# Seven of sixteen v units of attention by seven block products, with v ahead of q in two head groups

## The chip, the cores and the metric

One core of a Trainium2 chip runs the whole kernel. The metric is the device time of one execution in microseconds (us), taken as the median of several runs.

## What is computed

A two-layer decoder trunk on 256 tokens of width 2048 in float32: a pooling mixer and a gated feed-forward layer, then attention and a second feed-forward layer, each followed by a layer norm. The change lies in attention. Cut to that:

```python
def dilated_attention(h, k, v, w_q, w_o):
    q = (h @ w_q).reshape(B_, S, N_HEADS, HEAD_DIM)        # 16 heads of 128
    for window, dil in DILATED_BRANCHES:                   # (128, 1), (512, 4), (2048, 16)
        o, lse = _dilated_branch(q, k, v, window, dil)     # softmax over allowed distances
        ...
    wts = jax.nn.softmax(jnp.stack(lses, axis=0), axis=0)
    o = jnp.sum(wts[..., None] * jnp.stack(outs, axis=0), axis=0)
    return o.reshape(B_, S, D_MODEL).astype(h.dtype) @ w_o

# in reference():
k_shared = (h @ shared_w_k).reshape(B_, S, N_HEADS, HEAD_DIM)
v_shared = (h @ shared_w_v).reshape(B_, S, N_HEADS, HEAD_DIM)
```

The kernel merges the three branches into one softmax whose weights count in how many branches a distance is allowed (`cnt`).

## The kernel before

**Units.** All large products are cut into units, kept in the list `units` and numbered by their place in it. A unit is one weight block of 512 x 512 with its matmuls, and perhaps a `post` that takes the finished sums out of PSUM. Every number is split into a high part of the type float32r and a low part, so a block costs three products (high-high, high-low, low-high). The tiles `raw`, `wh` and `wl` of a unit (number behind the name) are the loaded block, its high part, cast by ScalarE (L82), and its low part, subtracted on VectorE (L83).

**What sets the order.** The engines' programs are written out in the order in which `run_units` emits them; nothing is rescheduled. For each unit i it first issues the loads up to unit i + 5 on SP (three `raw` buffers) and the splits up to unit i + 3 (four `wh` and `wl` buffers), then the unit's matmuls, then what was put off with `later(n, ...)` until n units on, then the unit's `post`. Each engine's queue is in order, SP's too: a load or a move that waits holds up what stands behind it.

**Seven products.** In the feed-forward layers many down-projection blocks are done by seven products of half-blocks in place of eight (`mk_seven`, `split_sums`). Such a block is two entries in `units`: half "a" with three products and half "b" with four. It has one load but two splits, the first of which (L103 to L109) also forms sums of the weights in `raw`, the second (L96, L97) splits these. On the left side it needs four sums of blocks of the activations, made by `left_sums`. Its results lie in four PSUM banks, two of which (`s2`, `s3`) are added into the others' output by `early`.

**Attention.** There are four head groups hq of four heads. Before, each takes four units of k, four of q and four of v. `group` makes k and q units, with features on the partitions, `group_tm` makes v units, with tokens on the partitions. `scores` does two heads at a time: q times k on TensorE, then the softmax on VectorE and ScalarE, which gives the probabilities `p`. These have to be turned before they can multiply v. `blocks` does that for a pair of heads: VectorE turns 32 x 32 blocks into `pb` (one buffer), then SP issues sixteen DMAs, eight after each of the next two units, that move the blocks to their places in `pTs`. `outputs` then multiplies `pTs` with `vt`, the finished v, in two PSUM banks, and ScalarE and VectorE take these out to `o`. Head group 3 is turned on TensorE instead (`transposes`). PSUM has eight banks, given out by `bank`.

Of the kernel before, what the change touches and what calls it, by code (L numbers as in the profile page):

```python
# [9 lines left out]
F32 = mybir.dt.float32  # L10
F32R = mybir.dt.float32r
# [6 lines left out]
T = 256  # L18
P = 128
# [13 lines left out]
def trunk(ctx: ExitStack, tc: tile.TileContext, x, pool_w_in, pool_w_grp, pool_scale, pool_w_out,  # L33
# [86 lines left out]
    def later(n, fn):  # L120
        if n == 0:
            fn()
        else:
            pending.append([n, fn])
# [818 lines left out]
    scale = 1.0 / math.sqrt(P)  # L943
    qk, pr, oq, pT, vts = {}, {}, {}, {}, {}

    def v_post(c):
        def post(t, ps):
            if t == 0:
                vts[c] = pools["attn"].tile([P, 2, 512], F32, name="vt", tag="vt")
                A.copy(vts[c][:, 0, :], ps)  # L950
            else:
                V.tensor_copy(vts[c][:, 1, :], ps)
                if c == 3:
                    later(1, lambda: transposes(c, (0, 1)))
                    later(2, lambda: transposes(c, (2, 3)))
                later(2 if c == 3 else 4, lambda: outputs(c, (0, 1)))
                later(3 if c == 3 else 7, lambda: outputs(c, (2, 3)))
        return post

    def qk_post(nm, hq):  # L960
        def post(ps):
            later(2 if hq == 0 and nm == "k" else 0, lambda: evac(ps))

        def evac(ps):
            ap = pools["attn"]
            o = ap.tile([P, 4, T], F32, name=nm, tag=nm)
            qk[nm] = o

            if hq == 0 and nm == "k":
                norm_evac(ps, 4, lambda m: o[:, m, :])  # L970
            else:
                for m in range(4):
                    A.copy(o[:, m, :], ps[m][:, T:])
                    V.tensor_tensor(o[:, m, :], o[:, m, :], ps[m][:, :T], OP.add)
            if nm == "q":
                later(2, lambda: scores(hq, range(0, 2)))
                later(3, lambda: scores(hq, range(2, 4)))
                if hq < 3:
                    later(4, lambda: blocks(hq, (0, 1)))
                    later(7, lambda: blocks(hq, (2, 3)))  # L980
        return post

    def scores(hq, ms):
        ap = pools["attn"]
        for m in ms:
            ps = bank("s")
            q, k = qk["q"][:, m, :], qk["k"][:, m, :]
            PE.matmul(ps[:, 0:P], q[:, :P], k[:, :P], start=True, stop=True)
            PE.matmul(ps[:, P:3 * P], q[:, P:], k, start=True, stop=True)  # L989
# [4 lines left out]
            V.scalar_tensor_tensor(sf, ps[:, :3 * P], scale, nf, op0=OP.mult, op1=OP.add)  # L994
# [25 lines left out]
    def transposes(hq, ms):  # L1020
        t = turned(hq, ms)
        for m in ms:
            ps = bank("pT")
            s = pr.pop((hq, m))[0]
            for i in range(3):
                PE.transpose(ps[:, i * P:(i + 1) * P], s[:, i, :], ident)
            A.copy(t[:, m % 2], ps[:, :3 * P])


    def blocks(hq, ms):  # L1030
        two = pr.pop((hq, ms[0]))[2]
        pr.pop((hq, ms[1]))
        b = hp.tile([P, 6 * P], F32, name="pb", tag="h")
        V.transpose(b, two.rearrange("p h s k -> p (h s k)"))

        t = turned(hq, ms)
        to = t.rearrange("p h s -> p (h s)").rearrange("p (k a j) -> p a k j", k=6, a=4)
        fr = b.rearrange("p (k b j) -> p b k j", k=6, b=4)

        def move(rows):  # L1040
            for i in rows:
                for j in range(4):
                    nc.sync.dma_start(to[32 * j:32 * j + 32, i], fr[32 * i:32 * i + 32, j])

        later(1, lambda: move((0, 1)))
        later(2, lambda: move((2, 3)))

    def outputs(hq, ms):
        if ms[0] == 0:
            oq[hq] = quad_tile("o")  # L1050
        vt = vts[hq]
        for m in ms:
            hd = slice(m * P, (m + 1) * P)
            ps = bank("o")
            t = pT.pop((hq, m))
            PE.matmul(ps[:, :T], vt[:, 0, hd], t[:, :T], start=True, stop=False)  # L1056
            PE.matmul(ps[:, P:T], vt[:, 1, hd], t[:, T:], start=False, stop=True)
            A.copy(oq[hq][:, m, 0, :T], ps[:, :T])
            V.tensor_tensor(oq[hq][:, m, 1, :T], ps[:, :T], oq[hq][:, m, 0, :T].bitcast(F32), OP.subtract)  # L1059
# [150 lines left out]
```

## Time and profile before

| what | value |
|---|---|
| median of 3 runs | 2030.75 us (2029.47 to 2030.89) |
| the profiled execution's own time | 2030.49 us |
| its span, first to last instruction | 2028.6 us |
| TensorE matmul, busy | 2021.7 us, 100% |
| VectorE, busy | 1674.5 us, 83% |
| ScalarE, busy | 1257.2 us, 62% |
| granted TensorE clock, mean | 0.999 |

In the profile PE is TensorE, PEld its weight loads, DVE VectorE, ACT ScalarE, SP the engine that issues most DMAs (SPq its queue). A row of a timeline is: start in us from the span's start, duration in us, engine, line of the source, operation, written tile <- read tiles, shapes, and in brackets the idle time ahead with what ended it. A matmul's duration contains the pipeline, so consecutive matmuls overlap; the distance of their starts is what one costs. A row of groups ends with the count, the total in us and the mean in ns, then idle time ahead. DMA rows give the time from issue to landing.

### The profile page before, as it was taken

The page shows a single profiled execution, that of the slowest core. Times are in us where ns is not written, and L with a number is a line of the kernel's source. Part 1 is how long each engine was busy: PE and PEld are TensorE (multiplying, and loading weights), DVE is VectorE, ACT ScalarE, POOL GpSimd, SP SyncE. Part 2 cuts the span into 40 slices and gives each one's busy share as a digit, 9 for nine tenths or more (in the row PEclk, how much of TensorE's full clock was granted, in tenths as well). Part 3 has the DMA queues.
Part 4 walks back from the last instruction along what each step waited for, and adds up shares of the span by engine and source line. Part 5 has one row for each costly group of instructions (what it writes and reads, how often), then busy time and mean ns, then how long its engine had stood idle before and what let it go on. Part 6 is the DMA issues. An engine that isn't in the chain of part 4 may idle for free.

```text
span 2028.6 us, 31127 instructions
## 1 busy us (share of the span) xinstructions
PE 2021.7 (100%) x12496; PEld 1809.4 (89%) x12496; DVE 1674.5 (83%) x1998; ACT 1257.2 (62%) x1685; POOL 75.0 (4%) x111
## 2 busy tenths in 40 slices
PE   9999999999999999999999999999999999999999
PEld 8898988899889988889888888998899989989987
DVE  6859887899789999879756657787889888989898
ACT  5544686667766676657533444577667676667672
POOL 2000000000000001100000000000000000100100
PEclk9999999999999999999999999999999999999999
DMA  8565467666655757864566554557666756666665
GB/s 257 201 206 188 165 209 210 190 192 225 210 191 187 234 188 219 232 226 165 191 197 195 169 185 168 187 178 216 187 198 197 228 187 213 198 213 196 209 214 180
DMA packets 278305, 405.92 MB, mean 200 GB/s; under 512 B 80414, under 2 KB 95668, under 8 KB 277904
## 3 DMA queue, kind: packets, MB, share of 16 engines
q1 hardware_dynamic: 266144, 389.72, 57.9%
q0 software_dynamic: 11584, 13.55, 4.4%
q8 instruction: 98, 1.61, 0.3%
q10 hardware_dynamic: 432, 0.66, 0.1%
q14 instruction: 47, 0.39, 0.1%
HBM read 380.01 MB, written 2.10 MB: 188 GB/s over the span
## 4 chain that ended last, share of the span: by engine, by line
PE 99%; DMA 0%; SPq 0%; DVE 0%; ACT 0%; issue 0%; DVEq 0%
PE acc L165 43%; PE acc L166 22%; PE t L238 3%; PE t L239 3%; PE t L240 3%; PE acc L169 3%; PE acc L170 3%; PE acc L168 3%; PE s L228 3%; PE s L229 3%; PE s L227 3%; PE t L228 2%; PE t L227 2%; PE t L229 2%; PE s L989 0%; PE o L1056 0%
## 5 line engine op out<-in xcount | busy, mean ns | idle before, releaser
L165 PE MATMUL acc<-xc,wh 128*128 128x512 f32 x3264 | 1151.9, 396 | 0.0
L166 PE MATMUL acc<-xc,wl 128*128 128x256 f32 x3264 | 916.3, 281 | 0.0
L83 DVE TENSOR_TENSOR wl<-raw,wh 128x2048 fp32r<-128x2048 f32 (+2 forms) x320 | 692.4, 2168 | 248.4 <-ACT wh L82 243.9
L165 PEld LDWEIGHTS acc<-xc,wh 128*128 128x128 f32 x3264 | 616.0, 189 | 143.7 <-DVE o L1059 0.6
L82 ACT CAST wh<-raw 128x2048 fp32r<-128x2048 f32 (+2 forms) x320 | 578.1, 1812 | 225.7 <-PE acc L165 118.3
L166 PEld LDWEIGHTS acc<-xc,wl 128*128 128x128 f32 x3264 | 615.5, 189 | 0.5
L96 ACT CAST wh<-raw 128x1024 fp32r<-128x1024 f32 x112 | 117.4, 1053 | 150.2 <-DVE raw L107 134.1
L97 DVE TENSOR_TENSOR wl<-raw,wh 128x1024 fp32r<-128x1024 f32 x112 | 133.8, 1221 | 0.5 <-ACT wh L96 0.5
L103 ACT CAST wh<-raw 128x1024 fp32r<-128x1024 f32 x112 | 87.7, 832 | 41.2 <-PE acc L165 24.7
L106 DVE TENSOR_TENSOR wl<-raw,wh 128x1024 fp32r<-128x1024 f32 x112 | 101.9, 951 | 1.3 <-ACT wh L103 0.9
L586 ACT ACTIVATE c<-u,cv 128x256 f32<-128x256 f32 x172 | 89.5, 593 | 19.4 <-DVE f L649 8.2
L228 PE MATMUL t<-wl,g 128*128 128x256 f32 x328 | 92.2, 281 | 0.0
L227 PE MATMUL t<-wh,g 128*128 128x256 f32 x328 | 92.1, 281 | 0.0
L229 PE MATMUL t<-wh,g 128*128 128x256 f32 x328 | 91.9, 280 | 0.0
L271 POOL DMA_DIRECT2D ht<-w x24 | 20.3, 847 | 1808.1 <-ACT wh L103 1060.1
L577 ACT COPY u<-acc 128x256 f32<-128x256 f32 x164 | 54.0, 372 | 46.9 <-PE acc L166 46.8
L229 PE MATMUL s<-wh,xs 128*128 128x256 f32 x296 | 82.6, 279 | 0.0
L228 PE MATMUL s<-wl,xs 128*128 128x256 f32 x296 | 82.6, 279 | 0.0
L227 PE MATMUL s<-wh,xs 128*128 128x256 f32 x296 | 82.5, 279 | 0.0
L591 ACT ACTIVATE a<-u,cv 128x256 f32<-128x256 f32 x172 | 73.6, 500 | 12.3 <-DVE g L659 6.5
L591 ACT ACTIVATE u<-u,cv 128x256 f32<-128x256 f32 x172 | 73.5, 500 | 0.0
L109 DVE TENSOR_TENSOR raw<-raw 128x1024 f32<-128x1024 f32 x56 | 68.6, 1225 | 1.9
(279 smaller groups left out, 3444.8 us busy)
## 6 DMA issues: line engine op xcount, KB each, us to landing
raw<-in_ffn_w_up_dram SPq DMA_DIRECT2D x160, 1024.0 KB, 4.9
raw<-in_ffn_w_down_dram SPq DMA_DIRECT2D x80, 1024.0 KB, 5.1
raw<-in_pool_w_out_dram SPq DMA_DIRECT2D x16, 1024.0 KB, 5.0
raw<-in_shared_w_k_dram SPq DMA_DIRECT2D x16, 1024.0 KB, 5.1
raw<-in_attn_w_q_dram SPq DMA_DIRECT2D x16, 1024.0 KB, 5.3
raw<-in_shared_w_v_dram SPq DMA_DIRECT2D x16, 1024.0 KB, 5.9
raw<-in_attn_w_o_dram SPq DMA_DIRECT2D x16, 1024.0 KB, 5.0
raw<-in_pool_w_in_dram SPq DMA_DIRECT2D x12, 1024.0 KB, 5.6
```

What stands on the lines that cost most here:

```text
L82: A.copy(wh[i][:, s], r[:, s])
L83: V.tensor_tensor(wl[i][:, s], r[:, s], wh[i][:, s].bitcast(F32), OP.subtract)
L96: A.copy(h[:, :, n], r[:, :, n])
L97: V.tensor_tensor(l[:, :, n], r[:, :, n], h[:, :, n].bitcast(F32), OP.subtract)
L106: V.tensor_tensor(l[:, k, n], r[:, k, n], h[:, k, n].bitcast(F32), OP.subtract)
L165: PE.matmul(ps[m], h[:, k, c], q[:, k, :, :T], start=st, stop=False)
L166: PE.matmul(ps[m][:, :T], l[:, k, c], q[:, k, 0, :T], start=False, stop=sp and not shifted)
L227: PE.matmul(to, xh, h[:, k, n], start=opens and kk == 0, stop=False)
L228: PE.matmul(to, xh, l[:, k, n], start=False, stop=False)
L229: PE.matmul(to, xl, h[:, k, n], start=False, stop=ends and kk == 1)
L586: A.activation(c[:, m, :], u[:, m, 2:], AF.Identity, scale=cv[:, 2, j:j + 1], bias=cv[:, 3, j:j + 1])
L591: A.activation(to[:, m, :], u[:, m, i:i + T], AF.Copy, scale=cv[:, i, j:j + 1])
```

## The change

Seven of the sixteen v blocks (three each in head groups 1 and 2, one in group 3) become seven-product blocks. `v_sums` forms the left sums from the normalised stream H for blocks 1, 2 and 3, once, while head group 1's k runs; the float32 sums lie in the buffer of k, the split ones in two tiles of the pool of activations (`xsum`) and in small tiles. `v_early` puts what lies in the two additional banks into `vt` first, and `v_post` adds the other two. In head groups 1 and 2 the order of the units is k, v, q. The calls of `outputs` move from v's `post` to q's. For head group 1 `blocks` comes 3 and 6 units after q (before: 4 and 7) and `outputs` 10 and 11 units after it (for groups 0 and 2: 8 and 11).

```diff
     def v_post(c):
         def post(t, ps):
-            if t == 0:
-                vts[c] = pools["attn"].tile([P, 2, 512], F32, name="vt", tag="vt")
-                A.copy(vts[c][:, 0, :], ps)
+            v = v_tile(c)[t]
+            if c > 0:
+                V.tensor_tensor(v, v, ps, OP.add)
+            elif t == 0:
+                A.copy(v, ps)
             else:
-                V.tensor_copy(vts[c][:, 1, :], ps)
-                if c == 3:
-                    later(1, lambda: transposes(c, (0, 1)))
-                    later(2, lambda: transposes(c, (2, 3)))
-                later(2 if c == 3 else 4, lambda: outputs(c, (0, 1)))
-                later(3 if c == 3 else 7, lambda: outputs(c, (2, 3)))
+                V.tensor_copy(v, ps)
+            if t == 1 and c == 3:
...
+    def v_early(c):
+        def early(p16, p75):
+            v0, v1 = v_tile(c)
+            left, right = v0[:, :256], v0[:, 256:]
+            A.copy(left, p16[:, :256])
+            V.tensor_tensor(right, left, p16[:, 256:], OP.add)
+            V.tensor_tensor(v1[:, :256], right, p75[:, :256], OP.add)
+            V.tensor_tensor(right, right, p75[:, 256:], OP.add)
+            V.tensor_tensor(v1[:, 256:], v1[:, :256], p75[:, 256:], OP.add)
+        return early
+    def v_sums(q, then):
...
+        f = ap.tile([P, 4, T], F32, name="f", tag="k")
+        d = [f[:, i].rearrange("p (k t) -> p k t", k=2) for i in range(4)]
+        V.tensor_tensor(d[0], a21, a22, OP.add)
+        V.tensor_tensor(d[1], d[0], a11, OP.subtract)
+        V.tensor_tensor(d[2], a21, a11, OP.subtract)
+        V.tensor_tensor(d[3], a12, d[1], OP.subtract)
+        def rest():
+            if q < 3:
+                t = quad_tile("xsum")
+                vsums[q] = [[t[:, i, hl, :T].rearrange("p (k t) -> p k t", k=2) for hl in range(2)] for i in range(4)]
+                split_act(t, f)
+                then()
+                return
...
+        later(1, rest)
...
             if nm == "q":
                 later(2, lambda: scores(hq, range(0, 2)))
+                if hq < 3:
+                    later(4 - (hq == 1), lambda: blocks(hq, (0, 1)))
+                    later(7 - (hq == 1), lambda: blocks(hq, (2, 3)))
+                    later(10 if hq == 1 else 8, lambda: outputs(hq, (0, 1)))
+                    later(11, lambda: outputs(hq, (2, 3)))
                 later(3, lambda: scores(hq, range(2, 4)))
-                if hq < 3:
-                    later(4, lambda: blocks(hq, (0, 1)))
-                    later(7, lambda: blocks(hq, (2, 3)))
+                if hq == 0:
+                    later(4, lambda: v_sums(3, lambda: v_sums(1, lambda: v_sums(2, lambda: None))))
...
+    def v_group(hq):
+        js = (0, 1, 2, 3)
+        seven = {0: (), 1: (1, 2, 3), 2: (1, 2, 3), 3: (3,)}[hq]
+        group_tm(shared_w_v, rows4, 512 * hq, 512, xsrcs, v_post(hq),
+                 seven={j: (lambda j=j: vsums[j]) for j in js if j in seven}, early=v_early(hq))
+
     for hq in range(4):
         x0 = hq == 0
         group(shared_w_k, rows4, 512 * hq, 512, psrcs if x0 else xsrcs, qk_post("k", hq), mode="x" if x0 else "ab")
+        if hq in (1, 2):
+            v_group(hq)
         group(attn_w_q[0], rows4, 512 * hq, 512, xsrcs, qk_post("q", hq))
-        group_tm(shared_w_v, rows4, 512 * hq, 512, xsrcs, v_post(hq))
+        if hq in (0, 3):
+            v_group(hq)
```

Before, head group 1 is the units 206 to 209 (k), 210 to 213 (q) and 214 to 217 (v). Now it is 206 to 209 (k), 210 to 216 (v: 210 plain, then three pairs "a", "b") and 217 to 220 (q); head group 2 is 221 to 224 (k), 225 to 231 (v: 225 plain, then the pairs 226/227, 228/229, 230/231) and 232 to 235 (q).

**VectorE, head group 1's turnings.** `pb` is the turned pair, and `wl` with its number shows where in the units this stands. Before, from the last split ahead of the first turning to the second turning:

```order
L83 TENSOR_TENSOR wl220_10305<-raw220_10180,wh220_10304 128x2048
L1034 STREAM_TRANSPOSE pb_10332<-p_10213 128x768
L952 COPY vt_10335<-t1_10155 128x512
L83 TENSOR_TENSOR wl221_10341<-raw221_10241,wh221_10340 128x2048
L83 TENSOR_TENSOR wl222_10391<-raw222_10302,wh222_10390 128x2048
L83 TENSOR_TENSOR wl223_10437<-raw223_10338,wh223_10436 128x2048
L1034 STREAM_TRANSPOSE pb_10472<-p_10274 128x768
```

Now, the last rows ahead of the second turning (the first stands ahead of the second pair's scores and of the split of 227):

```order
L104 TENSOR_TENSOR raw228_10511<-raw228_10511 128x2x256
L106 TENSOR_TENSOR wl228_10646<-raw228_10511,wh228_10645 128x4x256
L106 TENSOR_TENSOR wl228_10646<-raw228_10511,wh228_10645 128x2x256
L107 TENSOR_TENSOR raw228_10511<-raw228_10511 128x2x256
L109 TENSOR_TENSOR raw228_10511<-raw228_10511 128x4x256
L97 TENSOR_TENSOR wl229_10691<-raw228_10511,wh229_10690 128x4x256 x2
L1090 STREAM_TRANSPOSE pb_10714<-p_10560 128x768
```

Before, the second turning stood behind three plain splits after the first; now it stands behind the two halves of block 228/229, with the score chain of the second pair, the second half of 226/227 and the copies of k ahead of them.

**SP, head group 1's moves and the loads among them** (`pTs` are the moves of one pair, eight in a row; `raw` with its number is a unit's load). Before:

```order
L1043 DMA pTs_10334<-pb_10332 32x6x32 x8
L72 DMA raw224_10388<-in_attn_w_q_dram 128x4x512
L1043 DMA pTs_10334<-pb_10332 32x6x32 x8
L72 DMA raw225_10434<-in_attn_w_q_dram 128x4x512
L72 DMA raw226_10475<-in_shared_w_v_dram 128x4x512
L1043 DMA pTs_10474<-pb_10472 32x6x32 x8
L72 DMA raw227_10541<-in_shared_w_v_dram 128x4x512
L1043 DMA pTs_10474<-pb_10472 32x6x32 x8
```

Now:

```order
L1099 DMA pTs_10556<-pb_10554 32x6x32 x8
L72 DMA raw230_10643<-in_shared_w_v_dram 128x4x512
L1099 DMA pTs_10556<-pb_10554 32x6x32 x8
L72 DMA raw232_10717<-in_attn_w_q_dram 128x4x512
L1099 DMA pTs_10716<-pb_10714 32x6x32 x8
L72 DMA raw233_10760<-in_attn_w_q_dram 128x4x512
L1099 DMA pTs_10716<-pb_10714 32x6x32 x8
L72 DMA raw234_10794<-in_attn_w_q_dram 128x4x512
```

The loads between the moves were those of units 224 to 227; now they are those of v's last pair (230) and of the q units 232 and 233, and load 234 stands behind all moves.

**VectorE, head group 1's outputs taken out of PSUM** (`o` on the right is the PSUM bank; `vt` is v). Before:

```order
L83 TENSOR_TENSOR wl225_10544<-raw225_10434,wh225_10543 128x2048
L83 TENSOR_TENSOR wl226_10594<-raw226_10475,wh226_10593 128x2048
L83 TENSOR_TENSOR wl227_10632<-raw227_10541,wh227_10631 128x2048
L1059 TENSOR_TENSOR o_10513<-o_10667,o_10513 128x256
L1059 TENSOR_TENSOR o_10513<-o_10672,o_10513 128x256
L83 TENSOR_TENSOR wl228_10680<-raw228_10591,wh228_10679 128x2048
```

Now:

```order
L83 TENSOR_TENSOR wl232_10797<-raw232_10717,wh232_10796 128x2048
L83 TENSOR_TENSOR wl233_10827<-raw233_10760,wh233_10826 128x2048
L1115 TENSOR_TENSOR o_10848<-o_10849,o_10848 128x256
L1115 TENSOR_TENSOR o_10848<-o_10854,o_10848 128x256
L83 TENSOR_TENSOR wl234_10862<-raw234_10794,wh234_10861 128x2048
L1115 TENSOR_TENSOR o_10848<-o_10889,o_10848 128x256
L1115 TENSOR_TENSOR o_10848<-o_10894,o_10848 128x256
L972 TENSOR_TENSOR vt_10899<-vt_10899,s2_10656 128x256
```

Before, the second pair's outputs stood three units behind the first pair's, after unit 224 and behind the split of 227. Now the two pairs stand one split apart, after units 230 and 231, the second behind the split of 234, and the additions of v behind both.

More of the change, by code (lines that the diff above doesn't have):

```diff
@@ L958, in v_post @@
-        return post
+            v = v_tile(c)[t]
[3 more added lines that the diff above has]
+                A.copy(v, ps)
+            else:
+                V.tensor_copy(v, ps)
+            if t == 1 and c == 3:
+                later(1, lambda: transposes(c, (0, 1)))
+                later(2, lambda: transposes(c, (2, 3)))
+                later(2, lambda: outputs(c, (0, 1)))
+                later(3, lambda: outputs(c, (2, 3)))
+        return post
@@ new lines, in v_early @@
+    def v_early(c):
[8 more added lines that the diff above has]
+        return early
+    vsums = {}
+    def v_sums(q, then):
+        ap = pools["attn"]
+        x = H[q]
+        a11, a12, a21, a22 = (x[:, k:k + 2, t * P:t * P + P] for k, t in ((0, 0), (2, 0), (0, 1), (2, 1)))
+        f = ap.tile([P, 4, T], F32, name="f", tag="k")
[11 more added lines that the diff above has]
+                return
+            w = lnp.tile([P, 2, T], F32R, name="vs0", tag="fold2")
+            z = ap.tile([P, 2, T], F32R, name="vs3", tag="vs3")
+            vs = [[w[:, 0], w[:, 1]], [z[:, 0], z[:, 1]]]
+            for pair in (("S", "Q"), ("cs", "f1")):
+                vs.append([lnp.tile([P, T], F32R, name=f"vs{nm}", tag=nm) for nm in pair])
+            for i, v in enumerate(vs):
+                A.copy(v[0], f[:, i])
+            for i, v in enumerate(vs):
+                V.tensor_tensor(v[1], f[:, i], v[0].bitcast(F32), OP.subtract)
+            vsums[q] = [[u.rearrange("p (k t) -> p k t", k=2) for u in v] for v in vs]
+            then()
+        later(1, rest)
```

4 lines of the change are left out of this document (added).

## The prediction

> **What bounds the kernel now.** I read the page's busy times and its chain first.
>
> ```profile
> PE 2021.7 (100%) x12496; PEld 1809.4 (89%) x12496; DVE 1674.5 (83%) x1998; ACT 1257.2 (62%) x1685; POOL 75.0 (4%) x111
> PE 99%; DMA 0%; SPq 0%; DVE 0%; ACT 0%; issue 0%; DVEq 0%
> ```
>
> TensorE is never idle and the chain is TensorE alone. So a matmul taken away is worth the distance to the next one's start, and a wait put in front of TensorE costs its full length. The timeline of PE gives these distances: a seven-product unit of the feed-forward layer, a v unit (second and last matmul), a k unit (first matmul, and first of the next), an output block and a score block.
>
> ```profile
> 695.20 0.28 PE L227 MATMUL s<-wh,g 128*128 128x256 f32 x1
> 700.15 0.39 PE L165 MATMUL acc<-xc,wh 128*128 128x512 f32 x1
> ...
> 994.67 0.40 PE L239 MATMUL t<-wl,xc 128*128 128x512 f32 x1
> 999.79 0.39 PE L240 MATMUL t<-wh,xc 128*128 128x512 f32 x1
> 1000.01 0.39 PE L165 MATMUL acc<-xc,wh 128*128 128x512 f32 x1
> 1005.63 0.39 PE L165 MATMUL acc<-xc,wh 128*128 128x512 f32 x1
> 1022.53 0.59 PE L1056 MATMUL o<-pTs,vt 128*128 128x256 f32 x2
> 1024.08 0.28 PE L166 MATMUL acc<-xc,wl 128*128 128x256 f32 x1
> 1059.01 0.38 PE L988 MATMUL s<-k,q 128*128 128x128 f32 x2
> 1060.56 0.39 PE L239 MATMUL t<-wl,xc 128*128 128x512 f32 x1
> ```
>
> Seven products take 42 matmuls in 700.15 - 695.20 = 4.95 us, 0.118 each: 2.12 for the 18 of half "a", 2.83 for the 24 of half "b". A plain v unit takes 22 distances in 999.79 - 994.67 = 5.12, so 24 take 5.59. A k or q unit takes 1005.63 - 1000.01 = 5.62. An output block and a score block take 1.3 each (1.55 less the 0.23 of the matmul inside the bracket).
>
> **What goes.** Seven units at 5.59 - 4.95 = 0.64 us: **4.4 us less** on TensorE. This term is sure, since the same code runs in the feed-forward layer at this rate.
>
> **What comes on VectorE.** A plain unit costs it one subtraction, a seven-product unit eight operations.
>
> ```profile
> L83 DVE TENSOR_TENSOR wl<-raw,wh 128x2048 fp32r<-128x2048 f32 x280 | 640.4, 2289 | 234.5 <-ACT wh L82 230.3 <-DMA pTs<-pb 2.0 <-ACT wgb L444 1.7
> L97 DVE TENSOR_TENSOR wl<-raw,wh 128x1024 fp32r<-128x1024 f32 x112 | 133.8, 1221 | 0.5 <-ACT wh L96 0.5
> L109 DVE TENSOR_TENSOR raw<-raw 128x1024 f32<-128x1024 f32 x56 | 68.6, 1225 | 1.9
> L106 DVE TENSOR_TENSOR wl<-raw,wh 128x1024 fp32r<-128x1024 f32 x56 | 68.2, 1218 | 1.3 <-ACT wh L103 0.9
> L107 DVE TENSOR_TENSOR raw<-raw 128x512 f32<-128x512 f32 x56 | 38.8, 692 | 1.9
> L106 DVE TENSOR_TENSOR wl<-raw,wh 128x512 fp32r<-128x512 f32 x56 | 38.2, 683 | 0.0
> L104 DVE TENSOR_TENSOR raw<-raw 128x512 f32<-128x512 f32 x56 | 38.2, 682 | 0.0
> L286 DVE TENSOR_TENSOR xc<-h,xc 128x1024 fp32r<-128x1024 f32 x12 | 14.6, 1219 | 0.0
> L645 DVE TENSOR_TENSOR f<-c 128x256 f32<-128x256 f32 x17 | 7.1, 418 | 0.0
> L1059 DVE TENSOR_TENSOR o<-o 128x256 fp32r<-128x256 f32 x16 | 6.8, 425 | 22.2 <-ACT o L1058 22.2
> L974 DVE TENSOR_TENSOR k<-k,acc 128x256 f32<-128x256 f32 x12 | 4.2, 412 | 0.0
> L1034 DVE STREAM_TRANSPOSE pb<-p 128x768 f32<-128x768 f32 x6 | 5.8, 975 | 4.4 <-DMA pTs<-pb 4.4
> L82 ACT CAST wh<-raw 128x2048 fp32r<-128x2048 f32 x280 | 533.8, 1908 | 213.6 <-PE acc L165 114.6 <-issue 28.6 <-DMA raw<-in_ffn_w_down_dram 19.7
> ```
>
> Half "a" is 0.68 + 1.22 + 0.68 + 0.69 + 1.23 = 4.50, half "b" 2 x 1.22 = 2.44: 6.94 against 2.29, and more than the 4.95 that TensorE takes for the unit. Three in a row lose 6 us against TensorE; the lead of three units in the queue can hold that by itself. What can't be held is what stands behind it in program order: the turning of the probabilities, and the moves on SP.
>
> **Where TensorE comes to wait.** I set t = 0 at head group 1's first score block, after unit 222 (1059.01 in the trace of before). TensorE then has: score block to 1.3, unit 223 to 6.9, score block to 8.2, unit 224 to 13.85, unit 225 (plain v) to 19.4, 226 to 21.55, 227 to 24.4, 228 to 26.5, 229 to 29.3, 230 to 31.45, first output block to 32.75, 231 to 35.6, and here the second output block, which needs all sixteen moves of the second turned pair. The score chain on VectorE, from the timeline of DVE, for the two pairs:
>
> ```profile
> 1059.87 0.56 DVE L994 SCALAR_TENSOR_TENSOR p<-s,negm 128x384 f32<-128x384 f32 x1 [1.98 <-PE s L989]
> 1065.25 2.29 DVE L83 TENSOR_TENSOR wl<-raw,wh 128x2048 fp32r<-128x2048 f32 x1
> 1067.46 0.55 DVE L994 SCALAR_TENSOR_TENSOR p<-s,negm 128x384 f32<-128x384 f32 x1
> 1072.84 2.29 DVE L83 TENSOR_TENSOR wl<-raw,wh 128x2048 fp32r<-128x2048 f32 x1
> ```
>
> The first chain ends at 1065.25 - 1059.01 = 6.2; the second takes 5.4. VectorE's queue up to the second turning is then 6.2, half "a" of 226 4.5, first turning 1.0, second chain 5.4, half "b" 2.44, the copies of k 4 x 0.41 = 1.65, "a" of 228 4.5, "b" 2.44: 28.1. Neighbours overlap by some 0.07 us (1065.25 + 2.29 = 1067.54, but the next starts at 1067.46), so I take 27.3. It then takes 0.98, to 28.3. Now SP's queue:
>
> ```profile
> 1003.37 6.00 SPq L1043 DMA_DIRECT2D pTs<-pb  x8
> ...
> 1010.05 5.63 SPq L1043 DMA_DIRECT2D pTs<-pb  x8
> ...
> 1018.06 6.67 SPq L1043 DMA_DIRECT2D pTs<-pb  x8
> 1024.83 0.54 SPq L72 DMA_DIRECT2D raw<-in_shared_w_v_dram  x1
> 1025.42 6.49 SPq L1043 DMA_DIRECT2D pTs<-pb  x8
> DMA to landing us min/median/max: 1.8/4.1/6.7
> raw<-in_attn_w_q_dram SPq DMA_DIRECT2D x16, 1024.0 KB, 5.3
> ```
>
> Eight moves take 6.2 us of SP on the mean of these four rows, a weight load between them 0.6. So the second pair's moves issue from 28.3 to 34.5, load 233 to 35.1, the rest to 41.3; the last one starts at 40.7 and lands 1.9 later, near the least of the landing row: **42.6, where TensorE stands since 35.6: 7.0 us of waiting.** In the kernel before, the same sixteen moves had whole units of 5.6 us to land in.
>
> Behind it stands a second wait. Load 234 is next on SP: issued at 41.4, landed 5.3 later at 46.7, cast by ScalarE (1.91) at 48.6, subtracted (2.29) at 50.9. ScalarE's copy of the second output block stands behind that cast, VectorE's evacuation of it behind that subtraction: 0.43, so 51.3. And all eight PSUM banks are taken: v holds four until its sums are added, the outputs four. Unit 232 opens its four q banks in the outputs' banks, and its third one needs that evacuation. Without waits it would be reached at 35.6 + 1.3 + 2 x 0.35 = 37.6. So **both waits together delay TensorE by 51.3 - 37.6 = 13.7 us**, the second being 6.7 of it. After that, loads and splits are ahead again. The six additions that gather v (4 x 0.42 and 2 of the size of the copy below, 0.65: 3.0 us) come after this, or in group 1 while q's units run whose splits are three units ahead; without that cover they would cost their 3.0.
>
> **Smaller terms.** In head group 0 the same order reaches its second output block earlier too: after units 209 (until 1022.5), output block, 210, 211 and 212: 1022.5 + 1.3 + 5.6 + 2.1 + 2.8 = 1034.3.
>
> ```profile
> 1002.33 0.97 DVE L1034 STREAM_TRANSPOSE pb<-p 128x768 f32<-128x768 f32 x1
> 1003.22 0.65 DVE L952 COPY vt<-t 128x512 f32<-128x512 f32 x1
> ```
>
> VectorE goes from 1003.2 through three times four sums (12 x 0.42), four low parts (4 x 0.42), the copy 0.65, two subtractions (4.6), one low part of 1.22 and an "a" of 4.5, 17.7 us, 1020.0 with the overlaps; turning 1.0, moves and load 6.2 + 0.6 + 6.2, landing 1.3 more: 1035.3. **Wait 0.9**; I let it go from 0 to 2. Head group 2 and 3 have whole units around their turnings again, and the one seven-product unit of group 3 follows two plain ones: no wait.
>
> A waiting TensorE also loses its clock. The longest gap of before once matmuls run, on the PE timeline, and the granted clock (the column after POOL's) in the stretch that follows:
>
> ```profile
> 9.90 0.39 PE L168 MATMUL acc<-xc,wh 128*128 128x256 f32 x1 [1.57 <-ACT wh L82]
> 10.60:14.00 3.40, 3.37 (x16) 3.37 (x17) 1.32 (x2) 0.64 (x2) 0.00 (x0) 0.52 1.04 381
> ```
>
> After 1.57 us without a matmul the clock is about half for 3.4 us, which costs 1.7. The spell after the first wait falls inside the second wait; the one after the second counts: **1.7 us** (0 to 3.4). The row would also allow another 1.7 after the 0.9 us wait in head group 0; I put that in the upper end only. The Trainium skill, "TensorE: Matmul & The Clock Gate", Part 1, asks for a whole idle window of about 3.4 us before the clock falls; by that rule head group 0's wait adds nothing even if it grew to 2 us, and the sum stays as it is. The row of 1.57 us speaks against so long a window.
>
> **The sum.** -4.4 + 13.7 + 0.9 + 1.7 = +11.9 us. The profiled execution took 2030.49 (its span 2028.6 and 1.9 around it), 0.26 under the median of 2030.75: **2042.4 us**. Its low end: turning at 26.3, moves at 5.6, landing 4.6 for the load give 48.3 instead of 51.3, without clock and head group 0: 10.7 - 4.4 = +6.3. High end: turning at 28.1, moves at 7.2, landing 6.0 give 54.7, with 3.4 of clock and 2 and 1.7 of head group 0: 17.1 + 7.1 - 4.4 = +19.8.
>
> **Rivals.**
> 1. Only the moves are late. If load 234 came through before the moves, or unit 232's banks came free otherwise, the second wait drops: 7.0 + 0.9 + 1.7 - 4.4 = +5.2, 2035.7. Against it: SP issues in order, the load stands behind them. 0.12.
> 2. Faster: the moves and load 234 are in time, and the saving stays, 2030.49 - 4.4 = 2026.1. The point that decides is the start of the second turning: the delay follows it one to one, so for no delay it must start at 27.3 - 13.7 = 13.6, and for any gain by about 17. For it: in the feed-forward layer the same splits keep TensorE fed, with VectorE as loaded. Against it: there no transfer hangs on them, and the probabilities that are turned are only ready at the end of the second chain, 6.2 + 4.5 + 1.0 + 5.4 = 17.1, with four steps of VectorE still ahead of the turning. 0.06.
> 3. VectorE's deficit bites as well: two more waits of 2 us on split weights, each with its 1.7 us of clock, 11.9 + 7.4 = +19.3, 2049.8. For it: half "a" of unit 230 is ready at 28.3 + 0.7 + 1.2 = 30.2, with TensorE there at 29.3; this 0.9 falls inside the first wait. Against it: the other halves come 1 to 3 us ahead by the same sum. 0.08.
> 4. Waits of about the size of the saving, within 0.2% of before (4 us, what a measurement of this kernel can tell from no change): 0.02.
>
> **Chances.** The forecast keeps 0.72, slower with rivals 1 and 3: 0.92. The range goes from rival 1 to the high end without its last 1.3 us, 2035.5 to 2049.0; it leaves out rivals 2 and 4, and most of 3.
>
> **What would show it.** Right: two gaps of PE, 35.6 and some 44 us after head group 1's first score block, the first before an output matmul and released by a move, the second before unit 232's third bank and released by VectorE's evacuation of the outputs, with load 234 landing before it; granted clock under 1 there and nowhere else; L227 to L229 at 0.118 us each in attention. Wrong: no PE idle there (rival 2), or the gap ends with the first output (rival 1), or many short gaps on wl (rival 3).

## The result, and the profile after

The changed kernel takes 2040.32 us, the median of six runs (2039.67 to 2041.71), against 2029.28 us (2028.96 to 2030.89, six runs) of the kernel before on the same chip: a ratio of 1.0053, 95% interval 1.0040 to 1.0066. It is slower by about 11 us. The profiled execution took 2039.67 us, its span is 2037.8. Most of the difference lies in attention. Between the first and the last of the three matmuls of the norms' line L364, at about 160 and 1250 us of the span, the kernel before needs 1089.1 us and the changed one 1099.5: +10.4. I use this stretch below beside the medians, and call it the long stretch; it comes from one execution of each kernel.

The page of the changed kernel, its busy times:

```profile
PE 2020.5 (99%) x12622; PEld 1813.1 (89%) x12622; DVE 1717.5 (84%) x2073; ACT 1272.3 (62%) x1712; POOL 75.0 (4%) x111
```

TensorE's busy time fell by 1.2 us only, less than seven times 0.64, because matmuls at half clock count as busy; and it is no longer busy for the whole span. The chain, which was TensorE alone before, breaks off after a few per cent here and tells nothing. The waits of PE tell more (columns: what waited and for what, us in total, times, longest):

```profile
PE o L1112 <- DMA pTs<-pb: 4.9, 1, 4.9
PE acc L165 <- DVE o L1115: 4.8, 1, 4.8
```

Both are in head group 2, in the places that the prediction named. The timeline of PE, with the first matmuls of units 228 and 230 in front (1101.28 and 1106.24):

```profile
1076.78 0.38 PE L1044 MATMUL s<-k,q 128*128 128x128 f32 x2
1101.28 0.28 PE L227 MATMUL s<-wh,xc 128*128 128x256 f32 x1
1106.24 0.28 PE L227 MATMUL s<-wh,xc 128*128 128x256 f32 x1
1112.88 0.28 PE L229 MATMUL s<-wh,vsQ 128*128 128x256 f32 x1
1118.03 0.86 PE L1112 MATMUL o<-pTs,vt 128*128 128x256 f32 x2 [4.88 <-DMA pTs<-pb]
1120.74 0.80 PE L165 MATMUL acc<-xc,wh 128*128 128x512 f32 x1
1126.98 0.79 PE L165 MATMUL acc<-xc,wh 128*128 128x512 f32 x1 [4.80 <-DVE o L1115]
1127.79 0.63 PE L165 MATMUL acc<-xc,wh 128*128 128x512 f32 x1
1132.17 0.40 PE L165 MATMUL acc<-xc,wh 128*128 128x512 f32 x1
```

With t = 0 at 1076.78, head group 1's first score block, the first wait is from 36.4 to 41.25 and the second ends at 50.2. A pair of halves takes 1106.24 - 1101.28 = 4.96 us. The granted clock of these stretches (the column after POOL's) shows what the waits leave behind:

```profile
1119.00:1121.00 2.00, 1.86 (x7) 1.39 (x7) 2.00 (x3) 0.00 (x0) 0.00 (x0) 0.50 1.05 410
1127.00:1129.00 2.00, 2.00 (x6) 1.71 (x7) 1.93 (x6) 0.00 (x0) 0.00 (x0) 0.50 0.61 125
1133.00:1136.00 3.00, 3.00 (x19) 2.61 (x18) 0.00 (x0) 1.65 (x1) 0.00 (x0) 1.00 0.79 264
```

The other engines at this place, SP first, then ScalarE, then VectorE:

```profile
1104.73 5.58 SPq L1099 DMA_DIRECT2D pTs<-pb  x8
1110.40 0.54 SPq L72 DMA_DIRECT2D raw<-in_attn_w_q_dram  x1
1110.99 5.64 SPq L1099 DMA_DIRECT2D pTs<-pb  x8
1116.73 1.09 SPq L72 DMA_DIRECT2D raw<-in_attn_w_q_dram  x2
```

```profile
1122.37 1.90 ACT L82 CAST wh<-raw 128x2048 fp32r<-128x2048 f32 x1 [3.80 <-DMA raw<-in_attn_w_q_dram]
1124.17 0.64 ACT L1114 CAST o<-o 128x256 fp32r<-128x256 f32 x2
```

```profile
1103.69 0.97 DVE L1090 STREAM_TRANSPOSE pb<-p 128x768 f32<-128x768 f32 x1
...
1108.89 2.41 DVE L97 TENSOR_TENSOR wl<-raw,wh 128x1024 fp32r<-128x1024 f32 x2
...
1124.30 2.29 DVE L83 TENSOR_TENSOR wl<-raw,wh 128x2048 fp32r<-128x2048 f32 x1 [3.29 <-ACT wh L82]
1126.51 0.75 DVE L1115 TENSOR_TENSOR o<-o 128x256 fp32r<-128x256 f32 x2
```

The reader sees one chain. The second turning is at 26.9. The moves keep SP until 1116.6. Load 234 goes out behind them at 1116.73 and lands at 1122.4; its cast, its subtraction (the L83 at 1124.30), and only then the evacuation of the second outputs at 1126.51 (their copying out of PSUM by VectorE). The first part of that evacuation frees the bank that TensorE takes at 1126.98.

### The profile page after: what moved, and what is told of

Its sections match the earlier page's. It is cut to its first block, busy times and chain, and to the rows that moved or that the text cites. A ratio compares the mean times of both kernels' runs of the same rounds, so it can differ in the third digit from the quotient of the medians.

```text
span 2037.8 us, 31493 instructions
## 1 busy us (share of the span) xinstructions
PE 2020.5 (99%) x12622; PEld 1813.1 (89%) x12622; DVE 1717.5 (84%) x2073; ACT 1272.3 (62%) x1712; POOL 75.0 (4%) x111
## 5 line engine op out<-in xcount | busy, mean ns | idle before, releaser
L83 DVE TENSOR_TENSOR wl<-raw,wh 128x2048 fp32r<-128x2048 f32 (+2 forms) x313 | 676.1, 2166 | 227.7 <-ACT wh L82 223.8
L82 ACT CAST wh<-raw 128x2048 fp32r<-128x2048 f32 (+2 forms) x313 | 564.9, 1809 | 213.8 <-PE acc L165 119.8
L96 ACT CAST wh<-raw 128x1024 fp32r<-128x1024 f32 x126 | 131.8, 1053 | 166.9 <-DVE raw L107 141.4
L97 DVE TENSOR_TENSOR wl<-raw,wh 128x1024 fp32r<-128x1024 f32 x126 | 150.5, 1221 | 1.0 <-ACT wh L96 1.0
L103 ACT CAST wh<-raw 128x1024 fp32r<-128x1024 f32 x126 | 98.7, 832 | 41.3 <-PE acc L165 24.6
L106 DVE TENSOR_TENSOR wl<-raw,wh 128x1024 fp32r<-128x1024 f32 x126 | 114.7, 951 | 1.4 <-ACT wh L103 1.2
L109 DVE TENSOR_TENSOR raw<-raw 128x1024 f32<-128x1024 f32 x63 | 77.2, 1225 | 2.1
```

The lines of the kernel that those rows point to most:

```text
L82: A.copy(wh[i][:, s], r[:, s])
L83: V.tensor_tensor(wl[i][:, s], r[:, s], wh[i][:, s].bitcast(F32), OP.subtract)
L96: A.copy(h[:, :, n], r[:, :, n])
L97: V.tensor_tensor(l[:, :, n], r[:, :, n], h[:, :, n].bitcast(F32), OP.subtract)
L103: A.copy(h[:, k, n], r[:, k, n])
L106: V.tensor_tensor(l[:, k, n], r[:, k, n], h[:, k, n].bitcast(F32), OP.subtract)
```

## Experiments

The theory is the prediction's: seven-product units save their 0.64 us each on TensorE, and late moves, with a weight load behind them, cost more than that at one place. Rival A: the seven-product units cost by themselves, through VectorE's added work. Rival B: the order k, v, q costs. Rival C: only the wait for the moves counts. Rival D, for the second wait: the bank is late because the outputs are late. All runs are five rounds, each with the kernel before on the same chip; ratios are to that. They are told by question, not in order of time, so some texts ahead of a run speak of one that stands further down: the run with half the moves on GpSimd is halves, the second run of pe_out_9_10's text is pe_turn, and the run that gave 2027.8 is g1g3. Where a head group has only plain blocks, `v_post` copies v as before; the diffs leave that line out.

| run | median, us | ratio to before (95%) | long stretch, us |
|---|---|---|---|
| seven_g2 | 2042.29 | 1.0060 (1.0047 to 1.0073) | 1101.7 |
| order_g1 | 2029.87 | 1.0002 (0.9994 to 1.0011) | 1088.7 |
| g1g3 | 2027.84 | 0.9992 (0.9983 to 1.0001) | 1087.3 |
| pe_turn | 2032.20 | 1.0014 (1.0006 to 1.0023) | 1091.3 |
| pe_out_9_10 | 2027.41 | 0.9991 (0.9982 to 0.9999) | 1087.0 |
| out_10_10 | 2038.44 | 1.0045 (1.0032 to 1.0059) | 1096.8 |
| pool_moves | 2036.91 | 1.0038 (1.0026 to 1.0051) | 1094.7 |
| turn_sooner | 2043.45 | 1.0072 (1.0058 to 1.0086) | 1101.3 |
| halves | 2030.79 | 1.0006 (0.9997 to 1.0014) | 1089.7 |
| halves_9_9 | 2027.22 | 0.9989 (0.9980 to 0.9997) | 1085.6 |
| g2_kqv | 2043.63 | 1.0066 (1.0053 to 1.0078) | 1101.0 |

### Do the units save, and does the order cost?

**seven_g2**, fewer seven-product units under the same schedule:

```diff
-        seven = {0: (), 1: (1, 2, 3), 2: (1, 2, 3), 3: (3,)}[hq]
+        seven = {0: (), 1: (), 2: (1, 2, 3), 3: ()}[hq]
```

> The order k, v, q in head groups 1 and 2 and the schedule of turning, moves and outputs stay as in the changed kernel; only the three seven-product blocks of head group 2 are left, those of head groups 1 and 3 are plain again. Theory (each seven-product unit saves TensorE about 0.64 us; late moves, the weight load behind them and the half clock after them cost about 15 us at one place): the waits of 4.9 and 4.8 us stay as they are and four units give back 0.64 us each, so about 2.6 us above the changed kernel, 2042.9 (2041.5 to 2044). Rival A (the seven-product units cost by themselves, through VectorE's extra work, wherever they are): faster than the changed kernel, below 2039.

```profile
PE o L1112 <- DMA pTs<-pb: 4.6, 1, 4.6
PE acc L165 <- DVE o L1115: 4.3, 1, 4.3
```

The two waits stay, within half a microsecond, and the kernel is 2.0 us above the changed one (2042.29 against 2040.32, two sets of runs whose times overlap), the long stretch 2.2: about 0.5 us for each of the four units given up. The second wait also ends 0.6 us sooner after the first score block than in the changed kernel (1129.47 - 1079.89 = 49.6 against 50.2), so the four units may be worth up to 2.8 us, 0.7 each. Rival A asked for a faster kernel and falls.

**order_g1**, the order alone, and no seven-product unit (the call of `v_sums` is gone too):

```diff
-        if hq in (1, 2):
+        if hq in (1,):
             v_group(hq)
         group(attn_w_q[0], rows4, 512 * hq, 512, xsrcs, qk_post("q", hq))
-        if hq in (0, 3):
+        if hq in (0, 2, 3,):
             v_group(hq)
...
-        seven = {0: (), 1: (1, 2, 3), 2: (1, 2, 3), 3: (3,)}[hq]
+        seven = {0: (), 1: (), 2: (), 3: ()}[hq]
```

> No seven-product unit at all and none of their sums; only head group 1 in the order k, v, q, with the turning and the outputs at the changed kernel's units (head group 2 in k, q, v, as in the run that gave 2027.8 with four seven-product units). Theory: the order alone costs nothing where the outputs are late enough: 2029.3 (2028.3 to 2030.5). Rival B (the order costs by itself): 2030.5 or more, and then the four units of that run save more than 0.64 us each.

1.0002 with an interval that holds 1: the order of head group 1, its turning 3 and 6 units after q and the outputs at 10 and 11 cost nothing where whole units lie between. Rival B falls for head group 1. **g1g3** is the same order with `seven = {0: (), 1: (1, 2, 3), 2: (), 3: (3,)}` and the sums of `v_sums`:

> Head group 1 keeps the order k, v, q and its three seven-product units, head group 3 its one; head group 2 goes back to k, q, v with plain units, so head group 1's second output block stands about 10 us later on TensorE while its moves are issued at the same units. Theory: no wait for the moves, and none for a PSUM bank behind a late load; four units save 0.64 us each: 2029.3 - 2.6 = 2026.7 (2025.8 to 2028). Rival A (seven-product units cost by themselves): 2030 or more. Rival B (the order k, v, q costs by itself, in head group 1 too): 2031 or more.

1.1 us above the theory's number and inside its bounds. Both of these show no wait over 1.1 us on TensorE. Four units take 1.4 us off the long stretch and 2.7 off the span (2027.5 to 2024.8); by the medians the ratio falls by 0.0010, 2.0 us, with intervals that overlap. So the saving is there, and its size, 1.4 to 2.7 instead of 2.6, is not settled by this pair.

### Is it the moves?

**pe_turn**, the same units with no moves in head group 1:

```diff
-                    later(4 - (hq == 1), lambda: blocks(hq, (0, 1)))
-                    later(7 - (hq == 1), lambda: blocks(hq, (2, 3)))
+                    later(4 - (hq == 1), lambda: (transposes if hq == 1 else blocks)(hq, (0, 1)))
+                    later(7 - (hq == 1), lambda: (transposes if hq == 1 else blocks)(hq, (2, 3)))
```

> The whole change, but head group 1's probabilities are turned by TensorE (12 matmuls against the identity and four copies by ScalarE) and not by VectorE with 32 moves on SP's queue. Theory: both waits go, and with them the half clock; the 12 turnings cost TensorE 0.8 to 1.2 us per six, about 2.0 us: 2029.3 - 4.5 + 2.0 = 2026.8 (2026 to 2029). Rival A (VectorE's added work is what costs): within 2 us of the changed kernel, 2038 to 2041, since all its sums and seven-product units stay. Rival C (only the wait for the moves counts, the bank wait has another cause than the load behind the moves): about 2032 to 2034.

2032.20: 8.1 us faster than the changed kernel with every seven-product unit in place, so rival A falls again as the main cause; but 5.4 above the theory, and inside the 2032 to 2034 that I had given to rival C. Timelines of PE, SP, ScalarE and VectorE of this kernel, in that order:

```profile
1119.68 0.51 PE L165 MATMUL acc<-xc,wh 128*128 128x512 f32 x1 [3.20 <-DVE o L1115]
...
1120.99 0.63 PE L165 MATMUL acc<-xc,wh 128*128 128x512 f32 x1
```

```profile
1110.05 0.37 SPq L72 DMA_DIRECT2D raw<-in_attn_w_q_dram  x1
```

```profile
1115.06 1.91 ACT L82 CAST wh<-raw 128x2048 fp32r<-128x2048 f32 x1 [2.16 <-DMA raw<-in_attn_w_q_dram]
```

```profile
1107.61 2.41 DVE L97 TENSOR_TENSOR wl<-raw,wh 128x1024 fp32r<-128x1024 f32 x2
...
1117.00 2.29 DVE L83 TENSOR_TENSOR wl<-raw,wh 128x2048 fp32r<-128x2048 f32 x1 [1.23 <-ACT wh L82]
1119.20 0.75 DVE L1115 TENSOR_TENSOR o<-o 128x256 fp32r<-128x256 f32 x2
```

The wait for the moves is gone, the wait for the bank is not: 3.2 of 4.8 us are left. Load 234 lands 37.9 us after the first score block (1115.06 - 1077.21) instead of 45.6, so it is 7.7 us earlier without the moves. SP's queue had held it up by 5.4 of these: load 234 takes the buffer of block 230/231, which in the changed kernel is free when the last low parts of that block are done (the L97 there, until 1111.30), and it went out at 1116.73. Here it goes out at 1110.05, right behind the same low parts (until 1110.02). So without moves VectorE's own work on block 230/231 holds the load, and it still comes too late for the evacuation queued behind its split. Here the theory was incomplete: the second wait has a cause of its own, the order on VectorE, and rival C had that half right. The next two runs change that order alone.

**out_10_10**, the changed kernel with the second output block at unit 10:

```diff
-                    later(11, lambda: outputs(hq, (2, 3)))
+                    later(10 if hq == 1 else 11, lambda: outputs(hq, (2, 3)))
```

> The whole change, but head group 1's second output block is issued at unit 10 with the first, not at 11. Its moves are as late as before, so TensorE comes to it 3.1 us earlier and should wait 8.2 us instead of 4.9; but on VectorE its evacuation now stands ahead of the split of unit 234 (the third unit of the next q block), not behind it. Theory (the second wait, 4.8 us for a PSUM bank, is the evacuation queued behind that split): the second wait and its half clock go, one of 8.2 us is left: about 2040.3 - 3.2 = 2037 (2036 to 2039). Rival D (the bank is late because the outputs themselves are late, the split is not in the way): 2040 to 2044, both waits stay in sum and 3 us are added.

```profile
1122.79 1.19 PE L1112 MATMUL o<-pTs,vt 128*128 128x256 f32 x2 [8.56 <-DMA pTs<-pb]
```

```profile
1124.59 1.08 DVE L1115 TENSOR_TENSOR o<-o 128x256 fp32r<-128x256 f32 x3
...
1128.23 2.29 DVE L83 TENSOR_TENSOR wl<-raw,wh 128x2048 fp32r<-128x2048 f32 x1 [1.67 <-ACT wh L82]
```

The evacuations stand ahead of the split, the bank wait is gone, and the wait for the moves is 8.56, where 8.2 was expected. In the long stretch it is 2.7 us better than the changed kernel, by the medians 1.9, with times that overlap. Rival D asked for 2040 or more. This run alone doesn't settle it: the longer first wait also brings TensorE to the bank later. **pe_out_9_10** does the same without moves: pe_turn, with outputs at 9 and 10.

> Turning on TensorE as in the second run, without any moves, and the two output blocks at units 9 and 10 instead of 10 and 11, so that the second one's evacuation stands ahead of the split of unit 234 on VectorE. Measured with 10 and 11: 2032.2, with a wait of 3.2 us for the bank and about 2.3 us at half clock after it. Theory: both go, 2032.2 - 5.5 = 2026.7 (2025.5 to 2028.5). Rival D (the bank is late for another reason): within 1.5 us of 2032.2.

```profile
1115.09 2.28 DVE L83 TENSOR_TENSOR wl<-raw,wh 128x2048 fp32r<-128x2048 f32 x1
1117.29 0.75 DVE L1115 TENSOR_TENSOR o<-o 128x256 fp32r<-128x256 f32 x2
1118.58 2.29 DVE L83 TENSOR_TENSOR wl<-raw,wh 128x2048 fp32r<-128x2048 f32 x1 [0.54 <-ACT wh L82]
```

2027.41, 4.8 us off pe_turn: the wait of 3.2 and its half clock are gone. After the first score block (1078.83 here), TensorE reaches the third bank at 39.0 us and the split of 234 ends at 42.0; in pe_turn it was 39.3 and 42.1. So neither comes earlier or later, and only the place of the evacuation, ahead of the split, has changed: that the second wait is an evacuation queued behind a late split is shown.

**pool_moves**, the second pair's moves on GpSimd's queue, nothing else:

```diff
-                    nc.sync.dma_start(to[32 * j:32 * j + 32, i], fr[32 * i:32 * i + 32, j])
+                    (nc.gpsimd if hq == 1 and ms[0] == 2 else nc.sync).dma_start(to[32 * j:32 * j + 32, i], fr[32 * i:32 * i + 32, j])
```

> The whole change with its units as they are (second turning at unit 6, outputs at 10 and 11); only head group 1's second 16 moves go out on GpSimd's queue, not on SP's. In the run with half the moves there, GpSimd spent 0.56 us on each. Theory: the moves land about 16 x 0.56 + 2 us after the turning, some 2.7 us after TensorE comes for them (4.9 in the changed kernel); the load of unit 234 no longer stands behind them on SP, so the split ahead of the second evacuation is done at about the time that the outputs are, and the bank wait falls from 4.8 us to 0 to 1.5: 2029.3 - 4.5 + 2.7 + 0.8 + 2 (half clock) = 2030.5 (2029 to 2033). If the load behind the moves has no part in the second wait: 2036 or more.

The timeline of PE, and of the DMA issues those of the window from 1085 to 1130 us (the last column is the median from issue to landing, us), the last row from the same window of halves, which stands further down:

```profile
1123.49 1.19 PE L1112 MATMUL o<-pTs,vt 128*128 128x256 f32 x2 [7.55 <-DMA pTs<-pb]
```

```profile
pTs<-pb SPq DMA_DIRECT2D x16, 24.0 KB, 1.9
pTs<-pb POOLq DMA_DIRECT2D x16, 24.0 KB, 4.2
```

```profile
pTs<-pb POOLq DMA_DIRECT2D x16, 24.0 KB, 1.9
```

A miss: 6.4 us above my number. The bank wait is gone, as the theory had it, but the moves land later than I took: 4.2 us after issue at the median, not 2, so that the first wait is 7.55 and not 2.7. GpSimd's queue by itself is not the reason, since in halves its moves land in 1.9. In pool_moves two of q's loads, no longer behind the moves, go out beside them (at 1114.11 and 1116.99), and from 1116 to 1118 us the DMA engines are busy for 0.99 of the time; that the loads delay the moves is likely, but no run here shows it by itself. The time falls into the range that I had given to the opposite case, so the total alone would mislead; and since the longer first wait also gives the load time, this run does not show by itself what the load has to do with the second wait. The issue and landing times of load 234 under pe_turn do.

**turn_sooner**, the second turning two units sooner, all moves on SP:

```diff
-                    later(7 - (hq == 1), lambda: blocks(hq, (2, 3)))
+                    later(7 if hq != 1 else 4, lambda: blocks(hq, (2, 3)))
```

> The whole change, but the second turning stands two units sooner, so that on SP's queue the last 16 moves follow the first ones without a load between: they land about 5 us earlier, but the loads of units 232, 233 and 234 all stand behind 24 moves. Theory: the wait for the moves falls from 4.9 to 0 to 1 us, and what is won there is lost again to late loads (the first of them 11 us later than in the changed kernel, the third 4.5 us sooner): stalls of 4 to 8 us for splits or banks remain, 2036 (2033 to 2040). Rival C (only the wait for the moves counts): 2031 to 2033 with the bank wait unchanged at 4.8 or less.

Timelines of VectorE, SP and PE:

```profile
1102.23 0.98 DVE L1090 STREAM_TRANSPOSE pb<-p 128x768 f32<-128x768 f32 x1 [5.55 <-DMA pTs<-pb]
```

```profile
1095.02 19.61 SPq L1099 DMA_DIRECT2D pTs<-pb  x24
1114.73 10.03 SPq L72 DMA_DIRECT2D raw<-in_attn_w_q_dram  x4
```

```profile
1106.30 0.58 PE L228 MATMUL s<-wl,xc 128*128 128x256 f32 x1 [3.84 <-DVE wl L106]
1127.46 0.80 PE L165 MATMUL acc<-xc,wh 128*128 128x512 f32 x1 [6.46 <-DVE o L1115]
```

The wait for the moves is gone and the kernel is slower than the changed one, by 1.8 us in the long stretch. So rival C falls: removing that wait is worth nothing if the loads of units 232 to 234 pay for it. My forecast was wrong in sign: 2036 would have been faster than the changed kernel, and 2043.45 is 3.1 us slower. The trade of one wait for another came as described, but two costs were missing from my sum: the turning also had to wait 5.55 us for the first pair's moves, and the splits behind it on VectorE came late for TensorE by 3.84.

### Can the saving be kept?

**halves**: turn_sooner, with half of each pair's moves (`i >= 2`) on GpSimd's queue, and both output blocks at unit 10.

> The whole change with VectorE's turning kept; for head group 1 the second turning stands two units sooner (before the next combinations of v weights on VectorE), half of each pair's moves go out on GpSimd's idle queue, and both output blocks stand at unit 10. Theory: SP's last 8 moves end some 14 us sooner, no load stands behind 16 moves, both outputs' evacuations are ahead of the split of unit 234: no wait over 1 us, and the whole saving of seven units is left: 2029.3 - 4.5 = 2024.8 (2024 to 2027.5). Rival A (the seven-product units cost by themselves): 2030 or more. If GpSimd's moves take longer than the 0.85 us each of its other DMAs, the first wait comes back in part: up to 2032.

```profile
1119.66 0.79 PE L165 MATMUL acc<-xc,wh 128*128 128x512 f32 x1 [2.59 <-DVE o L1115]
...
1120.46 0.63 PE L165 MATMUL acc<-xc,wh 128*128 128x512 f32 x1
```

```profile
1114.78 4.49 DVE L83 TENSOR_TENSOR wl<-raw,wh 128x2048 fp32r<-128x2048 f32 x2 [0.57 <-ACT wh L82]
1119.19 1.41 DVE L1115 TENSOR_TENSOR o<-o 128x256 fp32r<-128x256 f32 x4
```

No wait for moves is left. VectorE ends the combinations of v's last weights at 1114.2, has two q splits next, and the outputs' evacuations behind both; TensorE waits 2.59 us for the first bank. My theory missed this, since I had looked at the split of unit 234 alone. The time lies in rival A's range (2030 or more), so the total can't tell the two apart; the next run can. **halves_9_9** puts both output blocks at unit 9, and so the evacuations ahead of the second of these splits.

> The run with half the moves on GpSimd and the second turning two units sooner, but both output blocks at unit 9, not 10, so that both evacuations stand on VectorE ahead of the split of unit 233 as well. Measured with unit 10: 2030.8, with 2.6 us of waiting for the bank and some 2.4 us at half clock after it. Theory (VectorE, behind on the combinations of head group 2's v weights, lets the evacuations wait behind two splits): both go, 2030.8 - 4.5 = 2026.3 (2025 to 2028.5). Rival: the wait is VectorE's backlog itself and only moves on to the split that is now later: 2029.5 to 2031.

```profile
1113.15 2.29 DVE L83 TENSOR_TENSOR wl<-raw,wh 128x2048 fp32r<-128x2048 f32 x1 [0.58 <-ACT wh L82]
1115.36 1.41 DVE L1115 TENSOR_TENSOR o<-o 128x256 fp32r<-128x256 f32 x4
1116.69 2.28 DVE L83 TENSOR_TENSOR wl<-raw,wh 128x2048 fp32r<-128x2048 f32 x1
```

2027.22, 0.9989 (0.9980 to 0.9997): the wait shrinks to 0.5 us, and this version is faster than the kernel before by 0.1% and than the changed one by about 13 us. In the long stretch the seven units bring 1088.7 - 1085.6 = 3.1 us against order_g1, of 4.4 worked out; 0.5 of the difference is this wait, the rest is open.

**g2_kqv** kept all seven units and moved only head group 2 back to k, q, v, with head group 1's outputs at 11 and 12.

> All seven seven-product units stay, and head group 1 in the order k, v, q; only head group 2 goes back to k, q, v, with head group 1's two output blocks 11 and 12 units after its last q unit, so that some 10 us more lie between the second 16 moves and the outputs that read them. Theory: both waits go and the whole saving is left: 2029.3 - 4.5 = 2024.8 (2024 to 2028; head group 2's v units now stand beside its own softmax, so VectorE may be late by 1 to 3 us there). Rival A: 2036 or more, since every seven-product unit stays.

Timelines of VectorE and PE:

```profile
1157.87 0.98 DVE L1090 STREAM_TRANSPOSE pb<-p 128x768 f32<-128x768 f32 x1 [4.68 <-DMA pTs<-pb]
1158.77 0.38 DVE L972 TENSOR_TENSOR vt<-vt,s 128x256 f32<-128x256 f32 x1
```

```profile
1161.17 1.19 PE L1112 MATMUL o<-pTs,vt 128*128 128x256 f32 x2 [8.48 <-DVE vt L955]
```

My largest miss, 19 us. Rival A's number came true but not its reason: the units themselves save, as the runs above show. With v behind q, head group 2's score chains stand between the combinations, its turning has to wait for the first pair's moves, and v's six additions stand behind that turning; TensorE waits 8.48 us for v. The order of head group 2 that costs nothing with plain units (order_g1 and g1g3 have it) leaves the kernel 14 us slower than before with seven-product ones. The order of the units and the kind of the units can't be judged apart.

## Why the prediction was right, and where not

The direction, the place and the mechanism came out, and the size within 2.1 us: 2042.4 foretold, 2040.32 measured. Step by step:

- **TensorE's saving**: 4.96 us for a unit in attention against 4.95 taken from the feed-forward layer. Right as a price of the unit (seven times 0.64 is 4.5, though, not 4.4); what reaches the end is 0.5 to 0.7 us a unit by seven_g2 and 3.1 us for all seven by halves_9_9.
- **Second turning**: foretold at 27.3, measured at 26.9. The sum over VectorE's queue holds.
- **Moves and first wait**: last landing foretold at 42.6, the outputs started at 41.25; TensorE came at 36.4, not 35.6. So 4.9 us of waiting, not 7.0. Mis-sized were the moves (5.6 us for eight, not 6.2: the least of the four rows shown, not their mean), and TensorE's own 0.8 us.
- **Load 234 and the third bank**: foretold at 51.3, measured at 50.2. Right in size, and its place in the queues is as described. Incomplete in cause: I took the load behind the moves for the whole reason. pe_turn has no moves and still waits 3.2 us, because the evacuation stands behind a split whose weights come late anyhow: their buffer is held by VectorE's work on block 230/231. So rivals 1 and 2 were priced as if the bank came free in time once the load did not stand behind the moves; taking the moves away gives 2032.2, not the 2026.1 of rival 2. Of that, turning on TensorE takes about 1.2 us (0.66 and 0.57 for six matmuls each, from their first start to the next matmul's), not the 2.0 that I had put into pe_turn.
- **The delay of both**: TensorE would have been at the third bank at 36.4 + 1.2 + 0.7 = 38.3, so 50.2 - 38.3 = 11.9 us, not 13.7.
- **Head group 0's second output block**: no wait, foretold 0.9, within its 0 to 2. It stands on the edge: with the same program there, TensorE waits 0.93 us for the moves in out_10_10 and 0.75 in pe_out_9_10.
- **Clock**: 5.0 us at half clock after the second wait, until about 1132. Eight pairs of matmuls take 0.64 instead of 0.35 us: 2.3 us, foretold 1.7 (0 to 3.4). That the spell after the first wait costs nothing was right too: the second output block took 2.71 us instead of 1.22, but the bank it leads to was waited for anyhow.

Sum with the measured sizes: -4.4 + 11.9 + 0 + 2.3 = +9.8, against +10.4 in the long stretch and +11.0 by the medians; with the 3.1 us of halves_9_9 in place of 4.4 it is +11.1. The forecast of the change, +11.9, was 0.9 us off; the rest of the 2.1 is the kernel before, 2029.28 in this set of runs and not 2030.49. That it came so close is in part luck: the waits were foretold too long by 1.8 and 0.9 us, the clock's loss too short by 0.6 and the saving too large. Rival 3, VectorE's deficit, did not show as short gaps on split weights; but it is what remains in pe_turn and halves once the moves are out of the way.

## What to carry to other kernels

A bank, a buffer or a queue that comes free late can have two things ahead of it in program order: ask of each separately what happens if the other is gone. Here one wait hid behind another, and taking away the first alone brought 8 us of 13, while putting two outputs one unit sooner brought another 5. Work that gives up TensorE time for another engine's time should be priced with what else stands in that engine's queue at that place: the same units gain 3 us or lose 14, by the order around them. When a rearranged step comes in time only by whole units, recount in microseconds, since shorter units move every "n units later" forward.

## What the runs showed of the hardware

Small moves between parts of SBUF (24 KB each) land at the median 2.0 us after issue from SP and 1.9 from GpSimd in halves. In pool_moves, SP's land in 1.9 and GpSimd's, beside weight loads, in 4.2; SP's own, with loads between them, took 4.1 in the kernel before. GpSimd takes 0.57 us for each issue (3.96 us for the last seven of pool_moves), SP in the same run 0.64 to 0.70 (5.14 and 5.58 for eight).

Two waits of 2.59 and 4.80 us were followed at once by matmuls at half clock; after the 3.20 us wait of pe_turn the first two pairs of matmuls still took 0.46 and 0.34 us, and the pair that starts at 1120.99 took 0.65. Runs whose longest waits are 1.1 to 1.3 us (pe_out_9_10, halves_9_9) show a mean granted clock of 1.0. The length of a gap does not decide alone: 1.75 us in seven_g2, at the place of the 1.57 us of the kernel before, left the clock at 1.00 (10 to 14 us), where that one was followed by half clock. The Trainium skill, "TensorE: Matmul & The Clock Gate", Part 1, speaks of a whole idle window of about 3.4 us before the clock falls; the gap of 2.59 us in halves, with half clock from its end, speaks against a window of that length that has to be idle as a whole, as the 1.57 us of the kernel before did.
